# Delta rule: block products cut to the rows and columns that are read, and squares summed into rows

## The chip, the core and the metric

The kernel runs on one core of one Trainium2 chip. Its time is device time in microseconds (us). Five engines work side by side, each through its own instructions in order: TensorE (PE; its weight loads are listed apart as PEld), VectorE (DVE), ScalarE (ACT), GpSimd (POOL) and SyncE (SP), which here only sends weight loads. They wait for each other through semaphores. Lower is better.

## The reference, cut to what matters

One decoder layer, 256 tokens, width 2048, all in float32. A combined input projection feeds softmax attention (8 heads) and a gated delta rule (8 query/key heads, 16 value heads, head dimension 128); both are projected, merged by gates and projected out, then normalised, and a SwiGLU feed-forward follows. A conditioning vector gives six modulation vectors through a 2048 x 12288 weight, `w_ada`. Two parts concern the change:

```
qb = l2norm(q) * 128**-0.5 ;  kb = l2norm(k)         # x * rsqrt(sum(x*x) + 1e-6), per token and head
L  = strictly lower part of (k_beta k^T) * decay     # per head and chunk of the sequence
A  = L + I
u, w = solve(A, [v_beta, k_beta * exp(g_cum)])       # unit lower triangular
```

The kernel uses two chunks of 128 tokens per head and inverts `A` (128x128, unit lower triangular) outright.

## The kernel before, in words

**Weights.** All large products are the same routine: a 512 KB block of weights is loaded (`load_w`, L204, sent by SP), split into a rounded high part (`hi`, ScalarE, L211) and a remainder (`lo`, VectorE, L212), and multiplied three ways (L289 to L291, L337 to L339, L296 and L300). Loads go through four buffers called `raw`. The same four buffers also take the blocks of `w_ada` (`raw_a`, L240), which VectorE multiplies and sums (L229).

**Order.** The program is a list of such weight steps, up to three loaded ahead. After each step a small planner, `tick`, lets background work advance in four lanes ("moba", "main", "pre", "ada"): each is a generator that yields its estimated cost, and a tick spends 1.8 of it; `yield rest(n)` sets a lane aside for n ticks. What is given out this way fixes the program order, from which a scheduler writes each engine's stream at build time. On the chip each engine follows its stream.

**The delta rule's background work** comes in two batches `b` of 8 value heads. Lane "pre" runs, per batch, the short convolutions, then `gdn_qk`: squares of the 8 query and key heads (L577, ScalarE), their sums over the 128 channels as products with a column of ones (L580), an inverse square root (`rsqrt`, L347 to L353, six VectorE instructions and a ScalarE square root), a scale (L583), a transpose on TensorE (L587), a copy (L589), and a transfer to DRAM (`rnd`, L590, POOL's queue). It is read back as a broadcast over partitions (`rb`, L595) and multiplied in on VectorE (L597).

Lane "main" runs `gdn_chain`: masked score matrices `ma0`, `ma1` (L636 to L642); the inversion of the 32x32 diagonal blocks on VectorE in 31 steps; a trip through DRAM that spreads the inverted blocks over 128 partitions as `UU` (the inverse, transposed) and `TT` (the inverse), L678; and then `pair`, which combines the blocks, 32 to 64 to 128, for two heads and two chunks at a time, and applies the result to the values. A helper `four` issues four products (L691); there are five calls per pair: M times T, the two products with U, again M times T, and the last with U. In between VectorE scales by beta into `z` (L700, L712) and ScalarE copies the blocks that are read back into `TT` and `UU` with a minus sign (L706, L707, L716). There are 8 pairs in all (2 batches, 2 halves, 2 pairs), and the two pairs of a half take turns. A float32 product is two instructions on TensorE, each with its weight load.

Of the kernel before, what the change touches and what calls it, by code (L numbers as in the profile page):

```python
# [10 lines left out]
F32 = mybir.dt.float32  # L11
F32R = mybir.dt.float32r
AF = mybir.ActivationFunctionType
OP = mybir.AluOpType
# [4 lines left out]
P = 128  # L19
D = 2048  # L20
S = 256
# [11 lines left out]
SCALE = HD ** -0.5  # L33
# [3 lines left out]
O_Z, O_B, O_A = 7168, 9216, 9232  # L37
O_GA, O_GB = 9248, 11296

C_ID, C_MASK, C_BA, C_SUM, C_TRI, C_END = 0, 128, 256, 288, 289, 545  # L40
V_ADA, V_LNG, V_LNB, V_CONV, V_END = 0, 96, 112, 128, 256


def constants():
    c = np.zeros((P, C_END), np.float32)
    i = np.arange(P)
    c[:, C_ID:C_ID + P] = np.eye(P)
    c[:, C_MASK:C_MASK + P] = np.where(i[None, :] >= i[:, None], 0.0, NEG)
    c[i, C_BA + i % 32] = 1.0
    c[:, C_SUM] = 1.0  # L50
    c[:, C_TRI:C_TRI + P] = i[:, None] <= i[None, :]
    c[:, C_TRI + P:] = -(i[:, None] > i[None, :]).astype(np.float32)
    return c
# [39 lines left out]
def layer(ctx, tc, a, out):  # L93
    nc = tc.nc
    v_, s_, g_, t_, dma = nc.vector, nc.scalar, nc.gpsimd, nc.tensor, nc.sync
    sdma = nc.gpsimd
# [5 lines left out]
    pt = ctx.enter_context(tc.tile_pool(name="pt", bufs=2, space=PSUM))  # L102
# [8 lines left out]
    def e2(nm, shape):  # L111
        return k1.tile(shape, F32, tag="e2", name=nm, bufs=3)
# [5 lines left out]
    cw = cols[:, V_CONV:V_END]  # L118
    ident = cst[:, C_ID:C_ID + P]
    mask = cst[:, C_MASK:C_MASK + P]  # L120
    ones = cst[:, C_SUM:C_SUM + 1]

    def load_x(k0, kn):
        dma.dma_start(x_sb[:, k0:k0 + kn, :], a["xT"][:, k0:k0 + kn, :])
# [38 lines left out]
    def rest(n=1):  # L163
        return -n
# [181 lines left out]
    def rsqrt(dst, e, r, src, eps_col):  # L346
        v_.tensor_scalar(e, src, eps_col, None, op0=OP.add)  # L347
        s_.activation(r, e, AF.Sqrt)
        v_.reciprocal(r, r)
        v_.tensor_tensor(dst, r, r, op=OP.mult)  # L350
        v_.tensor_tensor(dst, dst, e, op=OP.mult)
        v_.tensor_scalar(dst, dst, -0.5, 1.5, op0=OP.mult, op1=OP.add)
        v_.tensor_tensor(dst, r, dst, op=OP.mult)  # L353
# [8 lines left out]
    def c2(nm, shape):  # L362
        return k1.tile(shape, F32, tag="c2", name=nm, bufs=4)
# [207 lines left out]
    def gdn_qk(b):  # L571
        kq = kqs[b]
        yield rest()
        ss = pg.tile([P, 512], F32, tag="gd", name="ss")
        for t in range(0, 8, 2):
            sq = e2("sq", [P, 2, S])
            s_.activation(sq, kq[:, t:t + 2, :], AF.Square)  # L577
            for i in range(4):
                n = 2 * t + i
                t_.matmul(ss[:, n:n + 1], sq[:, i // 2, i % 2 * P:(i % 2 + 1) * P], ones, start=True, stop=True)  # L580
        n16 = k1.tile([P, 3, 16], F32, tag="n16", name="n16")
        rsqrt(n16[:, 0], n16[:, 1], n16[:, 2], ss[:, :16], epsc[:, 0:1])
        v_.tensor_scalar(n16[:, 0, :8], n16[:, 0, :8], SCALE, None, op0=OP.mult)  # L583
        yield 1.2
        yield rest()
        tp = pt.tile([P, P], F32, tag="tp", name="tp")
        t_.transpose(tp[:16], n16[:, 0], ident)  # L587
        r = e2("rn", [16, P])
        s_.copy(r, tp[:16])  # L589
        sdma.dma_start(rnd[b].rearrange("t (h i) -> (t h) i", h=2), r)  # L590
        yield 0.1
        yield rest(2)
        for t in range(4):
            rb = e2("rb", [P, 2, S])
            sdma.dma_start(rb, bass.AP(tensor=rnd[b].tensor, offset=rnd[b].offset + t * S,  # L595
                                       ap=[[0, P], [4 * S, 2], [1, S]]))
            v_.tensor_tensor(kq[:, t::4, :], kq[:, t::4, :], rb, op=OP.mult)  # L597
            yield 0.6
# [14 lines left out]
    def gdn_chain(b):  # L613
# [61 lines left out]
        for hh in range(2):  # L675
            uu, tt = [k1.tile([P, 8, P], F32, tag="m4", name=x, bufs=3) for x in ("UU", "TT")]
            for w, dst in ((0, uu), (1, tt)):
                sdma.dma_start(dst, ubd[w][8 * hh:8 * hh + 8, :P, :].rearrange("u c i -> c u i"))  # L678
            yield rest(((9, 4), (20, 6))[b][hh])

            def pair(gq):
                hs = 4 * hh + 2 * gq
                us = slice(4 * gq, 4 * gq + 4)
                beta = bcs[:, 3:5, 8 * b + hs:8 * b + hs + 2].rearrange("p a h -> p h a")
                beta = beta.unsqueeze(3).to_broadcast([P, 2, 2, P])

                def four(lhs, rhs):
                    ps = pg.tile([P, 4, P], F32, tag="gd", name="ps4")
                    for n in range(4):
                        lt, rt = lhs(n), rhs(n)  # L690
                        t_.matmul(ps[:lt.shape[1], n, :], lt, rt, start=True, stop=True)  # L691
                    return ps

                def M(n):
                    return ma0[:, hs + n // 2, 1, 0:P] if n % 2 == 0 else ma1[:, hs + n // 2, 1, :]

                U, T = uu[:, us, :], tt[:, us, :]
                ps = four(M, lambda n: T[:, n, :])
                z = c2("z", [P, 4, P])
                v_.tensor_tensor(z.rearrange("p (h a) i -> p h a i", a=2),  # L700
                                 ps.rearrange("p (h a) i -> p h a i", a=2), beta, op=OP.mult)
                yield 0.6
                ps = four(lambda n: U[:, n, :], lambda n: z[:, n, :])
                ps2 = four(lambda n: z[:, n, :], lambda n: U[:, n, :])
                for lo, hi in ((slice(0, 32), slice(32, 64)), (slice(64, 96), slice(96, 128))):
                    s_.activation(T[hi, :, lo], ps[hi, :, lo], AF.Copy, scale=-1.0)  # L706
                    s_.activation(U[lo, :, hi], ps2[lo, :, hi], AF.Copy, scale=-1.0)  # L707
                yield 0.1
                lo, hi = slice(0, 64), slice(64, 128)
                ps = four(M, lambda n: T[:, n, :])  # L710
                z = c2("z", [P, 4, 64])
                v_.tensor_tensor(z[hi].rearrange("p (h a) i -> p h a i", a=2),  # L712
                                 ps[hi, :, lo].rearrange("p (h a) i -> p h a i", a=2), beta[hi, :, :, lo], op=OP.mult)
                yield 0.35
                ps = four(lambda n: z[hi, n, :], lambda n: U[hi, n, :])
                s_.activation(U[lo, :, hi], ps[lo, :, hi], AF.Copy, scale=-1.0)  # L716
                yield 0.1

                hp = slice(hs, hs + 2)
                vn = c2("vn", [P, 2, 2, P])  # L720
                ps = pg.tile([P, 2, P], F32, tag="gd", name="pv0")
                for i in range(2):
                    t_.matmul(ps[:, i, :], U[:, 2 * i, :], bv[:, 0, hs + i, :], start=True, stop=True)
                s_.copy(vn[:, 0], ps)
                ps = pg.tile([P, 2, P], F32, tag="gd", name="pr1")
                for i in range(2):
                    t_.matmul(ps[:, i, :], ma0[:, hs + i, 1, P:S], vn[:, 0, i, :], start=True, stop=True)
                for i in range(2):
                    hd = 8 * b + hs + i
                    v_.scalar_tensor_tensor(bv[:, 1, hs + i, :], ps[:, i, :], nb[:, 1, hd:hd + 1], bv[:, 1, hs + i, :],  # L730
                                            op0=OP.mult, op1=OP.add)
                yield 0.4
                ps = pg.tile([P, 2, P], F32, tag="gd", name="pv1")
                for i in range(2):
                    t_.matmul(ps[:, i, :], U[:, 2 * i + 1, :], bv[:, 1, hs + i, :], start=True, stop=True)
                s_.copy(vn[:, 1], ps)
                po = pg.tile([P, 2, 2, P], F32, tag="gd", name="po")
                for i in range(2):
                    t_.matmul(po[:, 0, i, :], ma0[:, hs + i, 0, 0:P], vn[:, 0, i, :], start=True, stop=True)
                for i in range(2):  # L740
                    t_.matmul(po[:, 1, i, :], ma0[:, hs + i, 0, P:S], vn[:, 0, i, :], start=True, stop=False)
                    t_.matmul(po[:, 1, i, :], ma1[:, hs + i, 0, :], vn[:, 1, i, :], start=False, stop=True)
                s_.copy(bv[:, :, hp, :], po)
                yield 0.3

            pairs = [pair(0), pair(1)]
            while pairs:
                for x in list(pairs):
                    try:
                        yield next(x)  # L750
                    except StopIteration:
                        pairs.remove(x)
                yield rest()
# [490 lines left out]
```

## Time and profile before

| | |
|---|---|
| median of 3 runs | 1789.39 us (1779.66 to 1791.91) |
| the profiled execution | 1785.36 us |
| its span, first to last instruction | 1783.6 us |
| mean granted TensorE clock | 0.983 |
| ScalarE, POOL busy | 815.2 us (46%), 49.9 us (3%) |
| HBM read | 412.27 MB |

The profile is of one execution. "Busy" counts the time in which an engine has an instruction in work; matmuls are pipelined, so one lasts longer than the step to the next. An engine's idle time matters only where something on the chain of waits hangs on it. The granted clock is a share of 2.4 GHz; 0.5 is 1.2 GHz.

### The profile page before, as it was taken

The page shows a single profiled execution, that of the slowest core. Times are in us where ns is not written, and L with a number is a line of the kernel's source. Part 1 is how long each engine was busy: PE and PEld are TensorE (multiplying, and loading weights), DVE is VectorE, ACT ScalarE, POOL GpSimd, SP SyncE. Part 2 cuts the span into 40 slices and gives each one's busy share as a digit, 9 for nine tenths or more (in the row PEclk, how much of TensorE's full clock was granted, in tenths as well). Part 3 has the DMA queues.
Part 4 walks back from the last instruction along what each step waited for, and adds up shares of the span by engine and source line. Part 5 has one row for each costly group of instructions (what it writes and reads, how often), then busy time and mean ns, then how long its engine had stood idle before and what let it go on. Part 6 is the DMA issues. An engine that isn't in the chain of part 4 may idle for free.

```text
span 1783.6 us, 28261 instructions
## 1 busy us (share of the span) xinstructions
PE 1686.6 (95%) x11149; PEld 1537.1 (86%) x11149; DVE 1249.9 (70%) x1786; ACT 815.2 (46%) x1118; POOL 49.9 (3%) x68
## 2 busy tenths in 40 slices
PE   3899999999989999899999899999999999999995
PEld 3899999979989788889998899888888888888895
DVE  6899988888856787657875677676666655455454
ACT  3544445667433445336344344544444444433342
POOL 0000000110100001000000000000000000000001
PEclk9999999999999999999999999999999999999998
DMA  9999887666677577876876647777777755765652
GB/s 356 331 339 353 345 310 227 199 196 189 205 238 238 186 237 247 271 239 206 296 265 222 191 129 245 251 252 239 238 246 232 242 193 192 258 197 188 197 185 82
DMA packets 115158, 421.56 MB, mean 236 GB/s; under 512 B 13456, under 2 KB 14384, under 8 KB 109392
## 3 DMA queue, kind: packets, MB, share of 16 engines
q1 hardware_dynamic: 110016, 402.21, 66.7%
q0 software_dynamic: 5008, 17.53, 3.7%
q8 instruction: 88, 1.44, 0.3%
q14 instruction: 46, 0.38, 0.1%
HBM read 412.27 MB, written 7.42 MB: 235 GB/s over the span
## 4 chain that ended last, share of the span: by engine, by line
PE 41%; issue 15%; DMA 8%; DVE 5%; ACT 1%; POOL 0%; POOLq 0%; DVEq 0%; ACTq 0%
PE mm L296 16%; PE mm L300 8%; DMA raw_a<-in_w_ada 4%; DVE lo L212 3%; PE mm L290 3%; PE mm L291 3%; PE mm L289 3%; PE mm L339 2%; PE mm L338 2%; PE mm L337 2%; DMA raw<-in_w_proj_gdn 2%; DMA raw<-in_w_in 1%; ACT hi L211 1%; PE ps L691 1%; DMA rb<-rnd 1%
## 5 line engine op out<-in xcount | busy, mean ns | idle before, releaser
L211 ACT CAST hi<-raw 128x1024 fp32r<-128x1024 f32 (+2 forms) x572 | 582.0, 1020 | 768.7 <-PE mm L339 210.7
L212 DVE TENSOR_TENSOR lo<-raw,hi 128x1024 fp32r<-128x1024 f32 (+2 forms) x572 | 672.8, 1183 | 286.1 <-ACT hi L211 282.1
L289 PE MATMUL mm<-s,hi 128*128 128x256 f32 x1184 | 338.9, 286 | 4.9 <-ACT hi L211 4.7
L291 PE MATMUL mm<-s,lo 128*128 128x256 f32 x1184 | 333.3, 283 | 6.3 <-DVE lo L212 6.2
L290 PE MATMUL mm<-s,hi 128*128 128x256 f32 x1184 | 332.5, 281 | 0.0
L296 PE MATMUL mm<-h,hi 128*128 128x512 f32 x1280 | 319.0, 391 | 0.0
L296 PEld LDWEIGHTS mm<-h,hi 128*128 128x128 f32 x1280 | 228.8, 188 | 39.5
L289 PEld LDWEIGHTS mm<-s,hi 128*128 128x128 f32 x1184 | 225.0, 190 | 10.8 <-ACT hi L211 7.5
L291 PEld LDWEIGHTS mm<-s,lo 128*128 128x128 f32 x1184 | 224.2, 190 | 9.4 <-DVE lo L212 8.5
L290 PEld LDWEIGHTS mm<-s,hi 128*128 128x128 f32 x1184 | 224.8, 190 | 0.4
L300 PEld LDWEIGHTS mm<-h,lo 128*128 128x128 f32 x1280 | 171.1, 188 | 13.2
L300 PE MATMUL mm<-h,lo 128*128 128x256 f32 x1280 | 174.1, 278 | 0.0
L337 PE MATMUL mm<-hi,ach 128*128 128x512 f32 (+1 forms) x440 | 152.6, 347 | 0.0
L338 PE MATMUL mm<-lo,ach 128*128 128x512 f32 (+1 forms) x440 | 152.5, 347 | 0.0
L339 PE MATMUL mm<-hi,acl 128*128 128x512 f32 (+1 forms) x440 | 152.5, 347 | 0.0
L229 DVE CUSTOM_DVE_ANT_0 raw_a<-raw_a,cb,cols 128x1024 f32<-128x1024 f32 x56 | 71.8, 1283 | 77.9 <-DMA raw_a<-in_w_ada 77.9
L229 DVE CUSTOM_DVE_ANT_0 raw_a<-raw_a,cb,ada_half 128x1024 f32<-128x1024 f32 x56 | 71.8, 1283 | 64.8 <-DMA raw_a<-in_w_ada 64.8
L229 DVE CUSTOM_DVE_ANT_0 r<-r,cb,cols 128x2048 f32<-128x2048 f32 x40 | 93.7, 2347 | 14.1 <-DMA r<-in_w_ada 14.1
L337 PEld LDWEIGHTS mm<-hi,ach 128*128 128x128 f32 x440 | 83.3, 189 | 10.4
L339 PEld LDWEIGHTS mm<-hi,acl 128*128 128x128 f32 x440 | 83.3, 189 | 10.4
L338 PEld LDWEIGHTS mm<-lo,ach 128*128 128x128 f32 x440 | 83.3, 189 | 10.1
L338 PE MATMUL mm<-lo,s 128*128 128x512 f32 x192 | 77.0, 401 | 2.2 <-DVE lo L212 2.2
(288 smaller groups left out, 2383.2 us busy)
## 6 DMA issues: line engine op xcount, KB each, us to landing
raw<-in_w_ffn_in SPq DMA_DIRECT2D x176, 512.0 KB, 4.3
raw<-in_w_in SPq DMA_DIRECT2D x168, 512.0 KB, 4.4
raw_a<-in_w_ada SPq DMA_DIRECT2D x112, 512.0 KB, 4.5
raw<-in_w_ffn_out SPq DMA_DIRECT2D x88, 512.0 KB, 4.3
r<-in_w_ada SPq DMA_DIRECT2D x40, 1024.0 KB, 7.6
raw<-in_w_proj_gdn SPq DMA_DIRECT2D x32, 512.0 KB, 4.5
raw<-in_w_out SPq DMA_DIRECT2D x32, 512.0 KB, 4.2
raw<-in_w_in SPq DMA_DIRECT2D x40, 384.0 KB, 5.8
```

The lines of the kernel that those rows point to most:

```text
L211: s_.copy(hi, raw)
L212: v_.tensor_tensor(lo, raw, hi.bitcast(F32), op=OP.subtract)
L229: v_.tensor_tensor_reduce(out=raw, in0=raw, in1=cb[:, n * part:n * part + n], scale=1.0, scalar=cols[:, col:col + 1] if first else h, op0= ...
L289: t_.matmul(o, hi[:, i, c], ah, start=(first and i == 0 and t == 0), stop=False)
L290: t_.matmul(o, hi[:, i, c], al, start=False, stop=False)
L291: t_.matmul(o, lo[:, i, c], ah, start=False, stop=(last and i == kn - 1 and t == 1))
L296: t_.matmul(box[t].rearrange("p (u i) -> p u i", u=2), hi[:, i, t * P:(t + 1) * P], both[k0 + i], start=(first and i == 0), stop=False)
L300: t_.matmul(box[t][:, :S], lo[:, i, t * P:(t + 1) * P], both[k0 + i][:, 0, :], start=False, stop=(last and i == kn - 1))
L337: t_.matmul(box[h], xh, hi[:, i, :], start=start, stop=False)
L338: t_.matmul(box[h], xh, lo[:, i, :], start=False, stop=False)
L339: t_.matmul(box[h], xl, hi[:, i, :], start=False, stop=stop)
L691: t_.matmul(ps[:lt.shape[1], n, :], lt, rt, start=True, stop=True)
```

## The change

Two places. In `gdn_qk` the sums of squares no longer use the squares as weights and one column of ones as moving data. The weights are now 8 columns of the constants, of which the one for head n is all ones (a window of a block of 15 columns that slides), and the squares of a head, 256 tokens, move; eight products add into one 8x256 tile, so the sums stand as rows. `rsqrt` then works on 8 partitions of 256 elements, the result goes to DRAM without transpose and copy, and one rest of the lane falls away.

In `pair` every product is restricted to the rows and columns that are read afterwards. The first, third and last calls compute 32 or 64 columns for the 32 or 64 partitions that matter; the pair of products with U works on 32x32 blocks. The planner's cost of the first step is 0.55 instead of 0.6.

```diff
-C_ID, C_MASK, C_BA, C_SUM, C_TRI, C_END = 0, 128, 256, 288, 289, 545
+C_ID, C_MASK, C_BA, C_SEL, C_TRI, C_END = 0, 128, 256, 288, 303, 559
-    c[:, C_SUM] = 1.0
+    c[:, C_SEL + 7] = 1.0
...
     def gdn_qk(b):
-        ss = pg.tile([P, 512], F32, tag="gd", name="ss")
+        ss = pg.tile([8, S], F32, tag="gd", name="ss")
         for t in range(0, 8, 2):
             sq = e2("sq", [P, 2, S])
             s_.activation(sq, kq[:, t:t + 2, :], AF.Square)
-            for i in range(4):
-                n = 2 * t + i
-                t_.matmul(ss[:, n:n + 1], sq[:, i // 2, i % 2 * P:(i % 2 + 1) * P], ones, start=True, stop=True)
-        n16 = k1.tile([P, 3, 16], F32, tag="n16", name="n16")
-        rsqrt(n16[:, 0], n16[:, 1], n16[:, 2], ss[:, :16], epsc[:, 0:1])
-        v_.tensor_scalar(n16[:, 0, :8], n16[:, 0, :8], SCALE, None, op0=OP.mult)
-        yield 1.2
-        yield rest()
-        tp = pt.tile([P, P], F32, tag="tp", name="tp")
-        t_.transpose(tp[:16], n16[:, 0], ident)
-        r = e2("rn", [16, P])
-        s_.copy(r, tp[:16])
-        sdma.dma_start(rnd[b].rearrange("t (h i) -> (t h) i", h=2), r)
-        yield 0.1
+            for n in (t, t + 1):
+                t_.matmul(ss, cst[:, C_SEL + 7 - n:C_SEL + 15 - n], sq[:, n - t, :], start=(n == 0), stop=(n == 7))
+        rn = e2("rn", [8, S])
+        rsqrt(rn, e2("rne", [8, S]), e2("rnr", [8, S]), ss, epsc[:8, 0:1])
+        v_.tensor_scalar(rn[:4], rn[:4], SCALE, None, op0=OP.mult)
+        sdma.dma_start(rnd[b], rn)
+        yield 1.9
         yield rest(2)
...
-                def four(lhs, rhs):
-                    ps = pg.tile([P, 4, P], F32, tag="gd", name="ps4")
+                def four(lhs, rhs, to=slice(0, P), w=P):
+                    ps = pg.tile([P, 4, w], F32, tag="gd", name="ps4")
                     for n in range(4):
-                        lt, rt = lhs(n), rhs(n)
-                        t_.matmul(ps[:lt.shape[1], n, :], lt, rt, start=True, stop=True)
+                        t_.matmul(ps[to, n, :], lhs(n), rhs(n), start=True, stop=True)
                     return ps
...
-                ps = four(M, lambda n: T[:, n, :])
-                z = c2("z", [P, 4, P])
-                v_.tensor_tensor(z.rearrange("p (h a) i -> p h a i", a=2),
-                                 ps.rearrange("p (h a) i -> p h a i", a=2), beta, op=OP.mult)
-                yield 0.6
-                ps = four(lambda n: U[:, n, :], lambda n: z[:, n, :])
-                ps2 = four(lambda n: z[:, n, :], lambda n: U[:, n, :])
-                for lo, hi in ((slice(0, 32), slice(32, 64)), (slice(64, 96), slice(96, 128))):
-                    s_.activation(T[hi, :, lo], ps[hi, :, lo], AF.Copy, scale=-1.0)
-                    s_.activation(U[lo, :, hi], ps2[lo, :, hi], AF.Copy, scale=-1.0)
+                q = [slice(32 * n, 32 * n + 32) for n in range(4)]
+                ps = pg.tile([P, 4, 32], F32, tag="gd", name="ps_mt")
+                for n in range(4):
+                    for lo, hi in ((q[0], q[1]), (q[2], q[3])):
+                        t_.matmul(ps[hi, n, :], M(n)[:, hi], T[:, n, lo], start=True, stop=True)
+                z = c2("z", [P, 4, 32])
+                for hi in (q[1], q[3]):
+                    v_.tensor_tensor(z[hi].rearrange("p (h a) i -> p h a i", a=2),
+                                     ps[hi].rearrange("p (h a) i -> p h a i", a=2), beta[hi, :, :, 0:32], op=OP.mult)
+                yield 0.55
+                ps = pg.tile([P, 2, 4, 32], F32, tag="gd", name="ps_a")
+                for n in range(4):
+                    t_.matmul(ps[q[1], 0, n, :], U[q[1], n, q[1]], z[q[1], n, :], start=True, stop=True)
+                    t_.matmul(ps[q[0], 1, n, :], z[q[1], n, :], U[q[1], n, q[1]], start=True, stop=True)
+                s_.activation(T[q[1], :, q[0]], ps[q[1], 0], AF.Copy, scale=-1.0)
+                ps2 = four(lambda n: z[q[3], n, :], lambda n: U[q[3], n, q[3]], q[2], 32)
+                s_.activation(U[q[0], :, q[1]], ps[q[0], 1], AF.Copy, scale=-1.0)
+                s_.activation(U[q[2], :, q[3]], ps2[q[2]], AF.Copy, scale=-1.0)
                 yield 0.1
                 lo, hi = slice(0, 64), slice(64, 128)
-                ps = four(M, lambda n: T[:, n, :])
+                ps = four(lambda n: M(n)[:, hi], lambda n: T[:, n, lo], hi, 64)
...
-                ps = four(lambda n: z[hi, n, :], lambda n: U[hi, n, :])
-                s_.activation(U[lo, :, hi], ps[lo, :, hi], AF.Copy, scale=-1.0)
+                ps = four(lambda n: z[hi, n, :], lambda n: U[hi, n, hi], lo, 64)
+                s_.activation(U[lo, :, hi], ps[lo], AF.Copy, scale=-1.0)
```

## Rows read from the trace of the kernel before

**Rows 1.** The page, busy us, share of the span and instructions of each engine.

```profile
PE 1686.6 (95%) x11149; PEld 1537.1 (86%) x11149; DVE 1249.9 (70%) x1786; ACT 815.2 (46%) x1118; POOL 49.9 (3%) x68
```

**Rows 2.** The page, the chain that ended last: shares of the span by engine.

```profile
PE 41%; issue 15%; DMA 8%; DVE 5%; ACT 1%; POOL 0%; POOLq 0%; DVEq 0%; ACTq 0%
```

**Rows 3.** The chain of waits, 480 to 820 us, shares of that stretch by line.

```profile
by line: DMA raw_a<-in_w_ada 18.6%; DVE lo L212 9.9%; issue 7.7%; DMA raw<-in_w_in 6.6%; PE mm L289 5.2%; PE mm L290 5.2%; PE mm L291 5.0%; PE ps L691 3.3%; DMA rb<-rnd 3.2%; DVE Ub L666 2.5%; DVE tm L664 2.4%; ACT hi L211 2.3%; PE mm L339 
```

**Rows 4.** Stretches: busy us of each engine, granted clock, DMA share, GB/s.

```profile
core 0: us, PE busy (x) PEld busy (x) DVE busy (x) ACT busy (x) POOL busy (x), PEclk, DMA share, GB/s
336.00:344.00 8.00, 8.00 (x42) 7.82 (x41) 3.67 (x10) 1.49 (x5) 0.47 (x1) 0.57 0.83 245
364.00:367.00 3.00, 0.13 (x3) 0.00 (x1) 1.78 (x4) 0.36 (x1) 1.45 (x3) 0.99 0.61 242
367.00:371.00 4.00, 4.00 (x12) 3.30 (x13) 3.60 (x7) 2.79 (x7) 0.38 (x1) 0.58 0.83 210
372.00:490.00 118.00, 114.35 (x843) 106.87 (x842) 106.78 (x222) 77.57 (x107) 10.70 (x13) 1.00 0.61 192
491.00:495.00 4.00, 4.00 (x38) 4.00 (x37) 2.43 (x3) 1.28 (x2) 0.00 (x0) 1.00 1.01 326
502.00:505.00 3.00, 0.00 (x0) 0.00 (x0) 2.90 (x11) 1.05 (x1) 0.00 (x0) 1.00 0.76 210
524.00:532.00 8.00, 8.00 (x41) 7.52 (x42) 4.54 (x6) 0.76 (x2) 0.00 (x0) 0.58 0.66 195
576.00:582.00 6.00, 6.00 (x52) 5.70 (x50) 2.43 (x3) 2.19 (x4) 0.37 (x1) 1.00 0.80 254
```

**Rows 5.** Timeline of TensorE: start us, length us, the one-column products.

```profile
332.50 2.74 PE L580 MATMUL ss<-cst,sq 128*128 128x1 f32 x24
```

**Rows 6.** Timeline, norms and what waits; in brackets idle before and releaser.

```profile
346.22 0.17 DVE L583 TENSOR_SCALAR n<-n 128x8 f32<-128x8 f32 x1
355.09 0.51 POOL L590 DMA_DIRECT2D rnd<-rn  x1 [11.02 <-ACT rn L589]
364.56 0.69 DVE L597 TENSOR_TENSOR kq<-kq,rb 128x512 f32<-128x512 f32 x1 [5.63 <-DMA rb<-rnd]
505.07 0.28 PE L587 MATMUL tp<-cst,n 128*16 128x128 f32 x1 [3.21 <-DVE n L583]
505.93 0.53 POOL L590 DMA_DIRECT2D rnd<-rn  x1 [15.84 <-ACT rn L589]
523.95 3.68 PE L691 MATMUL ps<-UU,z 64*64 64x128 f32 x16 [3.97 <-DVE z L712]
```

**Rows 7.** The chain of waits around 601 us: start, length, piece.

```profile
601.05 0.86 PE g L636 x2
```

**Rows 8.** VectorE by line and shape: busy us, mean ns, idle before.

```profile
L349 DVE RECIPROCAL n<-n 128x16 f32<-128x16 f32 x2 | 0.5, 248 | 0.0
L498 DVE RECIPROCAL bcs<-w 128x32 f32<-128x32 f32 x1 | 0.4, 352 | 0.0
L700 DVE TENSOR_TENSOR z<-ps,bcs 128x512 f32<-128x512 f32 x8 | 5.2, 683 | 0.0
L712 DVE TENSOR_TENSOR z<-ps,bcs 64x256 f32<-64x256 f32 x8 | 3.4, 428 | 0.6 <-PE ps L691 0.3
```

**Rows 9.** Timeline of TensorE: products of a pair, and the weight product behind.

```profile
508.69 1.06 PE L691 MATMUL ps<-z,UU 128*128 128x128 f32 x8
509.58 1.06 PE L691 MATMUL ps<-UU,z 128*128 128x128 f32 x8
...
801.74 1.08 PE L691 MATMUL ps<-UU,z 64*64 64x128 f32 x8 [0.63 <-DVE z L712]
802.76 0.38 PE L289 MATMUL mm<-s,hi 128*128 128x256 f32 x1
```

**Rows 10.** Weight loads by line and shape: busy us, mean ns, idle before.

```profile
L691 PEld LDWEIGHTS ps<-TT,ma 128*128 128x128 f32 x128 | 15.0, 192 | 0.0
L432 PEld LDWEIGHTS ps_ba<-hf,wba 128*32 128x32 f32 x32 | 1.5, 111 | 24.6 <-ACT hf L429 23.6
```

More of the change, by code (lines that the diff above doesn't have):

```diff
@@ L120, in layer @@
     mask = cst[:, C_MASK:C_MASK + P]
-    ones = cst[:, C_SUM:C_SUM + 1]
     def load_x(k0, kn):
@@ L708, in pair @@
+                s_.activation(U[q[0], :, q[1]], ps[q[0], 1], AF.Copy, scale=-1.0)
+                s_.activation(U[q[2], :, q[3]], ps2[q[2]], AF.Copy, scale=-1.0)
                 yield 0.1
                 lo, hi = slice(0, 64), slice(64, 128)
-                ps = four(M, lambda n: T[:, n, :])
+                ps = four(lambda n: M(n)[:, hi], lambda n: T[:, n, lo], hi, 64)
                 z = c2("z", [P, 4, 64])
                 v_.tensor_tensor(z[hi].rearrange("p (h a) i -> p h a i", a=2),
-                                 ps[hi, :, lo].rearrange("p (h a) i -> p h a i", a=2), beta[hi, :, :, lo], op=OP.mult)
+                                 ps[hi].rearrange("p (h a) i -> p h a i", a=2), beta[hi, :, :, lo], op=OP.mult)
```

## The prediction

> **What bounds the kernel now.** I read the page's busy table first: TensorE is busy 95% of the span, VectorE 70% [rows 1]. That share doesn't say what a microsecond of TensorE is worth here, so I went to the chain of waits. It is 41% TensorE, 8% transfers, 5% VectorE and 15% "issue" of the span [rows 2]. The delta rule's combination runs between 500 and 815 us; cut to 480 to 820 us, the chain is led by `w_ada` transfers with 18.6%, and the term to see is "PE ps L691", the products being rewritten: 3.3% of 340 us, 11.2 us on the chain [rows 3].
>
> Then the windows table: granted clock and TensorE's busy time in single stretches [rows 4]. Three things are to be seen. At 336 us the clock falls to half for most of 8 us though TensorE was never idle; what ran just before is 24 one-column products, 2.74 us long [rows 5]. At 364 and 520 us TensorE is idle for 3 and 4 us, and after each the clock is at 1.2 instead of 2.4 GHz for a while (mean 0.58 over 4 and 8 us). At 502 us it is idle for 3 us with no fall.
>
> The waits name the cause of the idle times [rows 6]. At 364 us VectorE has waited 5.63 us for `rb`, the broadcast read of the norms; the norms were only sent at 355.09 because their transpose sat a tick later on TensorE. At 505.07 the transpose itself waited 3.21 us for VectorE, holding all products behind it. At 523.95 the last products of a pair wait 3.97 us for `z`, queued on VectorE behind four multiplies that waited for `rb`.
>
> **The change part by part.**
>
> *Squares (twice, batch 0 and 1).* Removed: 16 products of one column, 32 instructions at 2.74/24 = 0.115 us, 3.7 us. Added: 8 products with 256 columns moving and 8 columns of weights, 16 instructions. A float product with 512 moving columns takes 0.86 us for its two instructions, 0.43 each [rows 7], so 256 columns cost 0.21: 3.4 us. That is -0.3 us each. The larger part is the clock: 8 us at 0.57 cost 8 x 0.43 = 3.4 us in batch 0. In batch 1 the same products left the clock at 1.00 [rows 4], so this is not certain; bounds are 0 and -3.4, and I take -3.4, because a full-rate stream takes the place of the one-column one and TensorE was busy on both sides of the fall. The Trainium skill, "TensorE: Matmul & The Clock Gate", section on the HAM oscillation, ties the fall to idle gaps of the engine; by that rule the fall at 336 us would belong to something else and this term would be 0. The row, busy at 100% before the fall, speaks against it.
>
> *Transpose, copy and one rest removed.* The norms go to DRAM as soon as VectorE has them. Batch 0: VectorE had them at 346.4, the old path sent them 8.7 us later [rows 6]. VectorE's work grows: the reciprocal took 0.248 us on 16 and 0.352 us on 32 elements [rows 8], 6.5 ns an element, so 1.8 us on 256; the six others at most 0.43 us by the row of 256 elements, in all 4.4 us against at most 7 x 0.25 = 1.7, so +2.7 us per batch. In batch 0 it is hidden by the 5.63 us in which VectorE waits anyway. The norms then leave at about 349, and the multiply (9.5 us behind the sending in the old path) could start near 358.5, where VectorE now begins to wait (364.56 - 5.63 = 358.9). On POOL's queue the sending stands ahead of the `rb` reads as before. So the idle 3 us at 364 and the 4 x 0.42 = 1.7 us of half clock after it go: -4.7 us. What is late next is the weight cast, one step ahead of its use. Bounds: 0 (the multiplies move forward by as much as the transfer does) and -4.7.
>
> Batch 1: the transpose's wait of 3.21 us on TensorE goes, but VectorE was busy for 2.90 of those 3 us [rows 4] and the weight products behind need its subtractions: I count a third, -1.0. Against it the norms leave at 505.93 + 2.7 - 0.7 for the two hops saved = 507.9, 2 us later; that transfer is on the chain, with `z`, the weight subtractions and a POOL load (`TT`) queued behind: +2.0. Net +1.0, bounds -3 and +4.
>
> *Block products.* Per pair 40 instructions now: 32 of 128x128 at (509.58 - 508.69)/8 = 0.111 us, and 8 of 64x64 that take 802.76 - 801.74 = 1.02 us with the change of shape, 0.13 us more than eight of the others [rows 9]. Together 4.6 us, for 8 pairs 37. Afterwards 56 instructions: 40 with 32 columns on both sides, 16 with 64. No row has both short. The upper end is 0.111 (one moving column still stepped at 0.115, so the weights' 128 columns set it); the lower is those columns' share, 0.028 for 32 and 0.055 for 64. A load of 32 columns lasts 0.111 us against 0.192 [rows 10], so length does fall with columns; I take 0.065, near the middle. 56 x 0.065 = 3.6 us, plus four changes of shape at 0.13 = 4.1. That saves 0.5 us per pair, 4 us in all; the ends are 40 x 0.028 + 16 x 0.055 = 2.0 us (saves 2.1 a pair with the shape changes, 17 us) and 6.2 + 0.5 = 6.7 us (costs 17 us). On the chain lie 11.2 of 37 us, 30%: -1.2, between -5 and +5. The same skill page, section "Back-to-back issue gap", gives 25 ns or 62 ns as least spacing, depending on the decode path. By 62 ns the pair would be 3.5 us, by 25 ns near my lower end; no row here shows either.
>
> *The rest.* `z` goes from one operation of 0.683 us to two of 128 elements, about 0.30 each by the two rows for 512 and 256 [rows 8]; ScalarE drops one of four copies per pair. VectorE waits there for `raw_a` (first on the chain, [rows 3]), which hides the 0.08 us per pair: 0; without that cover -0.6 us. The constants grow by 14 columns: nothing.
>
> **Sum:** -3.7 - 0.3 - 4.7 + 1.0 - 1.2 = -8.9 us. The profiled execution took 1785.4 us, so 1776.5; the median of the runs shown is 4.0 us higher and would give 1780.5. I predict 1779.
>
> **Rivals.**
> 1. *Absorbed.* The gains end at the next `w_ada` transfer or weight cast; only a part of the batch 0 terms stays: 0 to -4, 1782 to 1789. For it: transfers lead the chain from 480 on [rows 3]. Against: from 372 to 490 us TensorE is busy for 114 of 118 us at full clock [rows 4], so what batch 0 gains should arrive at 490. Chance 0.20.
> 2. *Short products are no shorter.* At 0.111 us each the pairs cost 17 us more of TensorE, a third to all of it on the chain: +5 to +17 in place of -1.2: 1785 to 1797. For it: the one-column row. Chance 0.10.
> 3. *Slower: the clock.* The one-column products preceded a fall with TensorE "busy"; a 32x32 product is a sixteenth of a 128x128 one, and if bursts of them do the same, each of three bursts in four half-groups costs 3.4 us: 12 x 3.4 = 41, less 9: 1817. It decides once more than 8 of the 12 bursts are followed by half clock. Against: the 64x64 products at 574 us are followed by a clock of 1.00 from 576 to 582 [rows 4], and weight products stand between the bursts. Chance 0.06.
> 4. *More.* With one rest fewer the `rb` wait at 520 us falls away too: 4.0 idle and 8 x 0.42 = 3.4 of half clock; and at the low price of the products, half of their 17 us counts, 7 more than summed: 1779 - 7.4 - 7 = 1765. For it: all of these stalls stand in line behind one transfer. Against: VectorE sends later in batch 1. Chance 0.14.
>
> My forecast has the remaining 0.50, with its own range of 1773 to 1784. The change not doing what it says is rival 2.
>
> **Numbers.** One per cent, about what a measurement of this kernel can tell from no change, is 18 us: faster means below 1771.5, slower above 1807.3 against the median. Faster: rival 4 and a little of the forecast, 0.15. Slower: rival 3, 0.06. Within: 0.79. Range 1763 to 1797, which takes in rivals 1, 2 and 4 and leaves out rival 3 and tails.
>
> **What would show it.** Right: no half clock at 336-344 us; POOL sends the norms of batch 0 before 351 us and VectorE's first `rb` wait there is under 3 us; the transpose's line is gone; the reciprocal lasts about 1.8 us; steps of the new products at 0.05 to 0.08 us, with whole pairs on TensorE near 4 us instead of 4.6. Wrong: a clock under 0.9 behind the bursts, steps of 0.11 us, an `rb` wait in batch 1 over 6 us, or a batch 0 stretch that is as long as before because `lo` or a weight transfer ends it.

## The result: 1776.6 us, half a per cent faster

The changed kernel takes 1776.57 us in the median of 14 runs (1771.03 to 1782.33), the kernel before 1786.18 in 14 runs beside them. The ratio is 0.9948, 95% interval 0.9935 to 0.9961: 9.3 us less at 1785 us. The sum said -8.9. The profiled execution took 1772.32 us, with a span of 1770.3. That the sum is right to half a microsecond is chance, as the experiments show: the products were wrong by 17 us and the rest of the sum by 16, in opposite directions. Below, a ratio is turned into microseconds as (ratio - 1) x 1785. By the intervals given, one such figure is uncertain by 2 to 4 us, and the difference of two by some 4.

The busy line and the chain by engine of the changed kernel, to be held against [rows 1] and [rows 2]:

```profile
PE 1665.7 (94%) x11243; PEld 1509.8 (85%) x11243; DVE 1256.1 (71%) x1794; ACT 814.7 (46%) x1109; POOL 50.3 (3%) x68
...
PE 37%; issue 16%; DMA 6%; DVE 5%; ACT 1%; POOL 0%; POOLq 0%; ACTq 0%; DVEq 0%
```

TensorE lost 20.9 us of busy time, over twice what the time gained. The next view shows where the products lost it: TensorE by line and shape (busy us, mean ns of one, idle before), first the five calls of `pair` in the changed kernel, then the lines of the kernel before that they replace.

```profile
L682 PE MATMUL ps<-TT,ma 128*64 128x64 f32 x64 | 5.8, 261 | 0.1
L682 PE MATMUL ps<-UU,z 64*64 64x64 f32 x64 | 4.6, 221 | 1.2 <-DVE z L711 1.2
L682 PE MATMUL ps<-UU,z 32*32 32x32 f32 x64 | 3.8, 203 | 0.7 <-DVE z L696 0.7
L702 PE MATMUL ps_a<-UU,z 32*32 32x32 f32 x64 | 3.8, 202 | 0.0
L693 PE MATMUL ps_mt<-TT,ma 128*32 128x32 f32 x128 | 2.8, 197 | 1.7 <-DMA TT<-ubd 1.7
```

```profile
L691 PE MATMUL ps<-TT,ma 128*128 128x128 f32 x128 | 15.7, 275 | 0.0
L691 PE MATMUL ps<-z,UU 128*128 128x128 f32 x64 | 10.8, 321 | 7.7 <-DVE z L700 7.5 <-ACT TT L706 0.2
L691 PE MATMUL ps<-UU,z 64*64 64x128 f32 x64 | 9.9, 311 | 4.7 <-DVE z L712 4.6
L691 PE MATMUL ps<-UU,z 128*128 128x128 f32 x64 | 9.8, 304 | 0.0
```

Before it is 46.2 us. After, 20.8 in these lines and 3.7 in the other half of `ps_a` (L701): 24.5 together, 21.7 less. A mean of 200 ns is the length of one instruction, though, not the step to the next; the steps come from the timeline of TensorE in the changed kernel:

```profile
499.91 0.70 PE L693 MATMUL ps_mt<-TT,ma 128*32 128x32 f32 x32
554.31 0.41 PE L682 MATMUL ps<-UU,z 32*32 32x32 f32 x8 [0.23 <-DVE z L696]
511.99 1.15 PE L682 MATMUL ps<-TT,ma 128*64 128x64 f32 x16
517.31 1.14 PE L682 MATMUL ps<-UU,z 64*64 64x64 f32 x16 [1.15 <-DVE z L711]
```

32 instructions of `ps_mt` end 0.70 us after the first starts; less the length of one, (0.70 - 0.197) / 31 = 0.016 us a step. Eight 32x32 ones that all go to the same 32 partitions step at (0.41 - 0.203) / 7 = 0.030, the 64-column ones at about (1.15 - 0.22) / 15 = 0.062. `ps_a` alternates its output partitions as `ps_mt` does; its 16 instructions at 505.75 us take 0.44 us, (0.44 - 0.20) / 15 = 0.016 too. The steps of a pair are 32 x 0.016 + 8 x 0.030 + 16 x 0.062 = 1.7 us. For the old shapes the same count gives 40 x 0.111 = 4.4, and the prediction had 3.6 for the new ones; its 4.6 and 4.1 hold the changes of shape as well.

The other half of the story is in the windows. These are the stretches of batch 0 in the kernel before, where the rows ahead of the prediction did not look (TensorE, its loads, VectorE, ScalarE, POOL busy; granted clock; DMA share; GB/s):

```profile
344.00:360.00 16.00, 16.00 (x133) 15.78 (x132) 13.99 (x35) 10.89 (x22) 2.74 (x5) 1.00 0.65 218
360.00:368.00 8.00, 5.13 (x37) 4.81 (x36) 2.78 (x5) 2.24 (x5) 1.82 (x3) 0.93 0.71 226
416.00:440.00 24.00, 21.98 (x178) 21.10 (x177) 18.32 (x43) 20.20 (x32) 1.67 (x2) 1.00 0.57 179
344.00:488.00 144.00, 137.48 (x1005) 128.55 (x1004) 126.22 (x269) 93.12 (x138) 13.60 (x19) 0.99 0.62 196
```

And the same stretches of the changed kernel, with that of the old half clock first:

```profile
336.00:344.00 8.00, 8.00 (x63) 7.14 (x62) 4.97 (x11) 5.65 (x8) 0.00 (x0) 1.00 0.73 230
...
344.00:360.00 16.00, 8.93 (x69) 8.37 (x67) 10.46 (x25) 5.16 (x11) 3.70 (x6) 0.93 0.67 216
360.00:368.00 8.00, 8.00 (x50) 7.88 (x50) 6.15 (x14) 5.66 (x14) 1.32 (x3) 0.70 0.43 118
416.00:440.00 24.00, 19.55 (x163) 19.03 (x162) 19.09 (x50) 18.69 (x31) 2.24 (x3) 1.00 0.51 149
344.00:488.00 144.00, 130.57 (x945) 122.07 (x944) 122.92 (x261) 87.23 (x132) 16.36 (x21) 0.98 0.60 186
```

The half clock at 336 us is gone, the idle 2.9 us at 364 too. But TensorE is now idle for 7.1 us between 344 and 360, where it had been busy throughout, and 2.4 us longer between 416 and 440. Over batch 0's 344 to 488 us its idle time went from 6.5 to 13.4 us. The timeline of the changed kernel says on what it waits (in brackets the idle time and its releaser):

```profile
341.35 1.28 DVE L228 CUSTOM_DVE_ANT_0 raw_a<-raw_a,cb,ada_half 128x1024 f32<-128x1024 f32 x1 [2.96 <-DMA raw_a<-in_w_ada]
342.83 1.73 DVE L348 RECIPROCAL rnr<-rnr 8x256 f32<-8x256 f32 x1
349.24 0.53 POOL L582 DMA_DIRECT2D rnd<-rn  x1 [14.78 <-DVE e L622]
352.34 0.49 PE L822 MATMUL psS<-qk 128*128 128x128 f32 x2 [2.79 <-DVE ya L217]
358.53 0.69 DVE L589 TENSOR_TENSOR kq<-kq,rb 128x512 f32<-128x512 f32 x1 [5.19 <-DMA rb<-rnd]
359.33 0.29 DVE L838 TENSOR_SCALAR pe<-pe,st 128x128 f32<-128x128 f32 x1
359.67 0.47 PE L848 MATMUL tp<-cst,pe 128*128 128x128 f32 x1 [4.28 <-DVE pe L838]
434.56 0.70 PE L855 MATMUL poa<-pT,tv 128*128 128x256 f32 x2 [3.35 <-ACT pT L850]
```

The norms left at 349.24 and the multiply with `rb` ran at 358.53, both as predicted to within 0.3 us. Only VectorE's wait did not shrink (5.63 to 5.19): the multiply itself had moved a tick forward in VectorE's stream. In the kernel before, this wait stood ahead of `ya` (L218), and TensorE waited for that:

```profile
367.00 0.80 PE L823 MATMUL psS<-qk 128*128 128x128 f32 x2 [2.87 <-DVE ya L218]
```

Now it stands ahead of `pe` (L838), the division in the softmax of the attention that TensorE needs for the transposes of its next products, and TensorE waits 4.28 us in place of 2.87. The 2.79 us before it come from `ya` (L217), which VectorE delivers late; VectorE itself had waited 2.96 us for a block of `w_ada` (`raw_a`) at 341.35, in front of the reciprocal.

### The profile page after: what moved, and what is told of

Read it like the earlier page. It is cut to its first block, busy times and chain, and to the rows that moved or that the text cites. A ratio compares the mean times of both kernels' runs of the same rounds, so it can differ in the third digit from the quotient of the medians.

```text
span 1770.3 us, 28430 instructions
## 1 busy us (share of the span) xinstructions
PE 1665.7 (94%) x11243; PEld 1509.8 (85%) x11243; DVE 1256.1 (71%) x1794; ACT 814.7 (46%) x1109; POOL 50.3 (3%) x68
## 4 chain that ended last, share of the span: by engine, by line
PE 37%; issue 16%; DMA 6%; DVE 5%; ACT 1%; POOL 0%; POOLq 0%; ACTq 0%; DVEq 0%
PE mm L295 17%; PE mm L299 8%; DVE lo L211 3%; DMA raw<-in_w_in 2%; PE mm L338 2%; PE mm L337 2%; PE mm L336 2%; PE mm L289 2%; PE mm L290 2%; PE mm L288 2%; DMA raw<-in_w_proj_gdn 2%; DMA raw_a<-in_w_ada 1%; ACT hi L210 1%; DVE raw_a L228 0%; DVE Ub L658 0%
## 5 line engine op out<-in xcount | busy, mean ns | idle before, releaser
L336 PE MATMUL mm<-hi,s 128*128 128x512 f32 x192 | 78.4, 410 | 1.5 <-ACT hi L210 1.5
```

Of the source, the lines that this page charges most:

```text
L336: t_.matmul(box[h], xh, hi[:, i, :], start=start, stop=False)
```

## Experiments

The change has three parts that can be parted: the products, the squares' work, and the order (one rest of the lane lost, the sending a tick earlier). The order part also books the squares at a cost of 1.9 in place of 1.2 and 0.1, where a tick spends 1.8; "the lost rest" below is both, and no run parts them. All runs were compared with the kernel before.

**Products alone.** The kernel before with the new `pair`; squares, transpose and rests as before.

```diff
-                ps = four(M, lambda n: T[:, n, :])
+                ps = pg.tile([P, 4, 32], F32, tag="gd", name="ps_mt")
...
```

> The block products are cut, the squares stay as before. Theory A (the gain comes from the block products, whose step fell to about 0.016 us and so took some 24 us off TensorE): -7 to -11 us against before, nearly the whole gain. Theory B (the prediction's sum: squares and the earlier norms carry 8 of 9 us): -1 to -3 us. The clock at about 336 us falls to half again under both, if one-column products cause the fall.

1767.16 us, ratio 0.9899 (0.9881 to 0.9917): 18.0 us faster, twice the whole change and more than either theory had. That is the full 17 us that the prediction's lowest price gives and a little more, with no discount for what lies off the chain. The gain arises where the pairs run: VectorE's 157th `lo` (of 572, one for each weight block) comes at 470.6 us, before at 469.7; the 241st at 784.1, before at 804.5.

**Squares alone**, with the lost rest: the changed kernel with the old block of `pair`.

```diff
-                ps = pg.tile([P, 4, 32], F32, tag="gd", name="ps_mt")
+                ps = four(M, lambda n: T[:, n, :])
...
```

> The squares are summed by selector columns and a rest falls away, the block products stay wide. Theory A: between -2 and +2 us against before. Theory B: -7 to -9 us. Both: no half clock right behind the squares of batch 0, a reciprocal of 1.74 us, and an `rb` wait of VectorE of about 5 us that has only moved forward.

1792.3 us, 1.0036 (1.0022 to 1.0051): 6.4 us slower, which neither theory had. So this half of the change costs time, though it removes instructions.

**The lost rest alone.** The kernel before, with nothing but the two yields and the rest taken as in the changed kernel; the transpose stays.

```diff
-        yield 1.2
-        yield rest()
         tp = pt.tile([P, P], F32, tag="tp", name="tp")
...
-        yield 0.1
+        yield 1.9
```

> Before, with only the planner's yields of the squares changed (1.9 in place of 1.2, a rest and 0.1); same instructions, another order. Theory A: within 3 us of before, since order alone gives nothing. Rival C (what was gained is the order, one rest fewer): -5 to -10 us. The one-column products stay, so a fall of the clock behind them in batch 0 is expected again.

1795.97 us, 1.0053 (1.0035 to 1.0072): 9.5 us slower, with the same 11149 instructions on TensorE and 1786 on VectorE. Neither expectation had a loss. Two of the three stalls of the changed kernel are there, on the same releasers:

```profile
359.79 0.47 PE L847 MATMUL tp<-cst,pe 128*128 128x128 f32 x1 [4.12 <-DVE pe L837]
...
435.56 0.70 PE L854 MATMUL poa<-pT,tv 128*128 128x256 f32 x2 [4.09 <-ACT pT L849]
```

The wait for `ya` at 352 us is not; the reciprocal is still the short one here (L349 in [rows 8]), and VectorE doesn't wait for `raw_a` ahead of it.

**The changed kernel with one rest more ahead of the reads.**

```diff
-        yield rest(2)
+        yield rest(3)
```

> The changed kernel with three rests in place of two ahead of the `rb` reads, so that the multiplies stand one tick later in VectorE's stream. If the 5.2 us in which VectorE waits for `rb` in batch 0, the idle TensorE behind it and the half clock after it are on the path: -3 to -6 us against the changed kernel (-13 to -16 against before), and the wait under 3 us. If what batch 0 gains is taken back later: within 2 us of the changed kernel.

1770.33 us, 0.9923 (0.9902 to 0.9944), 4.5 us below the changed kernel by the ratios, hardly more than the intervals can tell. The multiplies go back a tick, and of the two stalls at 350 us the one behind `rb` nearly vanishes, while the one for `ya` stays:

```profile
352.92 0.76 PE L822 MATMUL psS<-qk 128*128 128x128 f32 x2 [2.75 <-DVE ya L217]
361.63 0.70 PE L848 MATMUL tp<-cst,pe 128*128 128x128 f32 x3 [0.79 <-DVE pe L838]
```

**Both parts with the old order.** The changed kernel; the sending stays a rest behind the norms.

```diff
+        yield 1.2
+        yield rest()
         sdma.dma_start(rnd[b], rn)
-        yield 1.9
+        yield 0.1
```

> The changed kernel with the planner's yields of the squares as before: 1.2, a rest, the sending, 0.1. If the lost rest alone is what the squares cost (the products alone gave -18 us, the lost rest alone +11): -18 to -22 us against before, as fast as the products alone or faster by the 3 us of half clock. If the row layout itself costs (2.7 us more on VectorE per batch): -12 to -16 us.

1760.55 us, 0.987 (0.985 to 0.9889): 23.2 us faster than before and 13.9 faster than the change, further than expected. It is the best version of this study; of both kernels it keeps the new work and the old order. Its windows for the same stretches:

```profile
344.00:360.00 16.00, 16.00 (x134) 15.82 (x133) 11.24 (x29) 8.00 (x18) 4.29 (x7) 1.00 0.60 187
360.00:368.00 8.00, 3.16 (x18) 2.77 (x17) 6.76 (x14) 4.42 (x10) 0.38 (x1) 0.81 0.64 197
416.00:440.00 24.00, 24.00 (x203) 23.84 (x202) 21.67 (x50) 20.23 (x35) 1.67 (x2) 1.00 0.63 202
344.00:488.00 144.00, 137.86 (x1007) 129.42 (x1006) 126.80 (x265) 91.78 (x138) 15.37 (x20) 0.98 0.62 195
```

TensorE is busy throughout from 344 to 360 and from 416 to 440 us. Over 344 to 488 us it is idle for 6.1 us, against 13.4 in the changed kernel. It pays 4.84 us at 366 us, more than the kernel before, and still comes out ahead. The reciprocal is the long one here too, but there is no wait for `ya`: the block of `w_ada` ahead of the reciprocal comes with hardly a wait.

```profile
336.88 1.28 DVE L228 CUSTOM_DVE_ANT_0 raw_a<-raw_a,cb,ada_half 128x1024 f32<-128x1024 f32 x1 [0.42 <-DMA raw_a<-in_w_ada]
340.37 1.74 DVE L348 RECIPROCAL rnr<-rnr 8x256 f32<-8x256 f32 x1 [0.38 <-ACT rnr L347]
366.05 1.22 PE L857 MATMUL poa<-pT,tv 128*128 128x256 f32 x2 [4.84 <-ACT pT L852]
```

**The squares' work with the old order**, and the old products: the changed kernel with both edits.

```diff
+        yield 1.2
+        yield rest()
         sdma.dma_start(rnd[b], rn)
-        yield 1.9
+        yield 0.1
...
-                ps = pg.tile([P, 4, 32], F32, tag="gd", name="ps_mt")
+                ps = four(M, lambda n: T[:, n, :])
...
```

> Wide block products, squares by selector columns, the planner's yields as before. Lost rest to blame: -4 to 0 us against before. Row layout to blame: +2 to +6 us, with VectorE's reciprocals of 1.74 us ahead of weight subtractions.

1781.46 us, 0.9987 (0.9973 to 1.0): 2.3 us faster, with no change at the edge of the interval. So the new squares are worth some 2 us alone and, by 0.9899 to 0.987, 5 on top of the new products, each hardly more than the intervals can tell. The lost rest on top of them costs 1.0036 - 0.9987, 8.7 us.

**Products alone, padded.** The first version, with 24 wide instructions of the old shape added per pair ahead of the small ones; their results are overwritten.

```diff
+                def wide():
+                    big = pg.tile([P, 4, P], F32, tag="gd", name="big")
+                    for n in range(4):
+                        t_.matmul(big[:, n, :], M(n), T[:, n, :], start=True, stop=True)
+                    return big
-                ps = pg.tile([P, 4, 32], F32, tag="gd", name="ps_mt")
+                ps = wide()[:, :, 0:32]
...
```

> The block products alone (as e1), and ahead of three of the five groups four wide products M times T into the same tile, whose result is overwritten: 24 instructions of 128x128 per pair, 2.7 us, so that a pair takes about 4.3 us of TensorE as before. If TensorE's time in the pairs is what counts: the gain of 18 us shrinks to 0 to 5. If it was the shorter hops on VectorE and ScalarE or the order: it stays at 12 to 18.

1785.74 us, 1.0003 (0.9989 to 1.0017). The busy time of TensorE rose from 1672.0 to 1695.7 us, by 23.7; the time by 18.6. Within the 2.5 us of the interval the whole gain is gone, though the smaller VectorE multiplies and the dropped copy are in the padded version too: what gained was TensorE's time in the pairs. By these two busy times it counts at 18.6 / 23.7 = 78%. The share is rough: from the kernel before to the products alone the busy time fell by 14.6 us and the time by 18.0, and the padded version is as fast as the kernel before with 9.1 us more of busy time. So a few microseconds may come from something else; no run parts them.

```profile
PE 1672.0 (95%) x11277; PEld 1520.8 (86%) x11277; DVE 1251.2 (71%) x1794; ACT 811.8 (46%) x1110; POOL 49.8 (3%) x68
```

```profile
PE 1695.7 (95%) x11469; PEld 1541.7 (86%) x11469; DVE 1248.2 (70%) x1794; ACT 812.7 (46%) x1110; POOL 49.9 (3%) x68
```

The first line is the products alone, the second the padded version.

**Both with the old order, sums as 32 rows of 64.** Four times as many selector products, each a quarter as wide; VectorE then works on 64 elements a partition, not 256.

```diff
-        ss = pg.tile([8, S], F32, tag="gd", name="ss")
+        ss = pg.tile([32, 64], F32, tag="gd", name="ss")
...
-                t_.matmul(ss, cst[:, C_SEL + 7 - n:C_SEL + 15 - n], sq[:, n - t, :], start=(n == 0), stop=(n == 7))
+            for n in range(4 * t, 4 * t + 8):
+                t_.matmul(ss, cst[:, C_SEL + 31 - n:C_SEL + 63 - n], sq[:, n // 4 - t, n % 4 * 64:n % 4 * 64 + 64],
+                          start=(n == 0), stop=(n == 31))
```

> As e5, with the sums laid out as 32 rows of 64 (a window of 63 selector columns, 32 products with 64 columns moving), so the reciprocal falls from 1.74 to about 0.55 us and VectorE's work for the norms from about 4 to 2 us per batch. If that work is on the path: 2 to 5 us faster than e5. If not: within 1.5 us of e5.

1766.29 us, 0.9898 (0.9881 to 0.9915): 5.0 us slower than the version with both and the old order, hardly more than the intervals can tell, where 2 to 5 faster was expected. The reciprocal did fall from 1.74 to 0.54 us, and the first multiply with `rb` came at 352.31 us instead of 357.58. That it lost all the same is not explained: the scheduler ordered other work differently as well, and no run here parts the two. The trace shows only where: the 157th `lo` comes at 470.9 us against 467.7 in the version with both, the 169th at 522.6 against 513.2.

**The old order in one batch only.** Batch 0 keeps the rest, batch 1 does not, and the mirror of it.

```diff
+        if b == 0:
+            yield 1.2
+            yield rest()
         sdma.dma_start(rnd[b], rn)
-        yield 1.9
+        yield 0.1 if b == 0 else 1.9
```

> The changed kernel with the old plan of the norms' step (cost 1.2, one rest, sending, cost 0.1) in batch 0 alone; batch 1 keeps the new one. Theory L (what the lost rest costs is one stall of batch 0, the attention products at 434 us that come a tick early and wait for the copy of pT): at the sigmoid near 500 us the changed kernel is 12.6 us behind the version with both rests, and at 585 us 14.5, so batch 0 holds some 13 of 16 us: 1762 to 1765, the pT wait under 1 us. Theory M (either batch costs half): about 1768. Theory N (batch 1 holds it): 1775 to 1778.

> The mirror: the old plan in batch 1 alone. Theory L: 1772 to 1776, the pT wait near 434 us still 3 to 4 us. Theory M: about 1768. Theory N: 1760 to 1763. If the two batches' shares don't add up to 16 us, the order of one depends on the other's.

Batch 0: 1764.3 us, 0.9887 (0.987 to 0.9903). Batch 1: 1771.4 us, 0.9922 (0.9901 to 0.9943). Against the changed kernel that is -10.9 and -4.6 us; together 15.5, where both at once gave 13.9. So the cost lies about two thirds in batch 0, and theory L has the larger share right. The wait for `pT` near 435 us is gone with batch 0's rest and still 3.37 us without it, as that theory has it, but it was one stall of three. TensorE's waits at 340 to 370 us, in batch 0 kept, then in batch 1 kept:

```profile
365.11 0.72 PE L858 MATMUL poa<-pT,tv 128*128 128x256 f32 x2 [3.86 <-ACT pT L853]
```

```profile
356.06 0.80 PE L825 MATMUL psS<-qk 128*128 128x128 f32 x2 [2.79 <-DVE ya L217]
363.01 0.47 PE L851 MATMUL tp<-cst,pe 128*128 128x128 f32 x1 [2.45 <-DVE pe L841]
```

With batch 0's rest both early stalls are gone and one later one is left; without it they are back. VectorE's 169th `lo` comes at 511.2 us here and at 513.2 in the version with both rests, where batch 0 keeps its rest; in the changed kernel and the mirror it comes at 526.5 and 529.0. The rest of batch 1 is worth 4.6 us by the mirror and 3.0 by 0.9887 to 0.987, about what the intervals can tell, and no single stall was found for it. The two traces can't show it: the mirror's profiled execution took 1776.68 us, the changed kernel's 1772.32, the other way round from their medians.

**The best version with a rest more ahead of the reads.**

```diff
         yield 0.1
-        yield rest(2)
+        yield rest(3)
```

> The version with both rests, with one more tick ahead of the broadcast reads (rest(3) in place of rest(2)). In that version VectorE still waits 4.58 us for rb in batch 0. If that wait matters, 2 to 4 us below that version's 1760.6: 1757 to 1759. If what matters is only where a tick puts the attention pieces of batch 0, this shifts them again, to either side: 1758 to 1772; above 1766 it speaks for the order and against the wait.

1770.91 us, 0.9923 (0.9907 to 0.9939): 9.5 us slower than without it. VectorE's first wait for `rb` did fall, from the first of these rows (the best version) to the second:

```profile
357.58 0.69 DVE L591 TENSOR_TENSOR kq<-kq,rb 128x512 f32<-128x512 f32 x1 [4.58 <-DMA rb<-rnd]
```

```profile
359.70 0.69 DVE L591 TENSOR_TENSOR kq<-kq,rb 128x512 f32<-128x512 f32 x1 [1.50 <-DMA rb<-rnd]
```

3 us of wait less and 9.5 us of time more: the length of that wait was not what mattered. TensorE's idle time from 344 to 488 us went from 6.1 to 12.3 us. The same extra rest gained 4.5 us in the changed kernel.

## Why the prediction came out right, point by point

By the ratios the change is: products -18.0, squares' work -5.2 on top of them, lost rest +13.9, in all -9.3. The prediction had -1.2, and -7.7 for squares and order together with their signs mixed. The total was right, two steps were not.

- *Squares.* Right in its row: 336 to 344 us runs at 1.00. 16 instructions took 3.4 us by prediction; the selector products' busy time for both batches is 7.2 us, 3.6 each. The price of -4.0 for both batches lies between the -2.3 and -5.2 that the runs give for the squares' whole work, transpose and longer `rsqrt` included.
- *Transpose, copy and rest.* This step failed, in taking -4.7 from two bounds that both excluded a loss: the rest that falls away costs 8.7 to 13.9 us. The multiply moved forward by as much as the transfer did, which the prediction had as its bound of 0; but what it moved ahead of, the softmax's division, was not looked for. "What is late next is the weight cast" was wrong: it was the attention. The other new stall, `ya`, shows near 352 us in the four traces with the new squares and no rest in batch 0 (2.75 to 2.86 us). In just these four VectorE has waited 2.95 to 3.03 us for a block of `w_ada` in front of the reciprocal; in the five with the new squares and that rest it waited 0.17 to 0.42 us there, and of these three have no wait for `ya` at that place and two have 0.35 and 1.18 us. So that stall takes the order and the new squares together, and the late block goes with it; that the longer VectorE work alone would bring it is not shown, and the three traces speak against it. Batch 1's net +1.0 had the bounds -3 and +4; its rest is worth 3.0 to 4.6 us.
- *Block products.* This step failed twice, both times too careful. The step was taken as 0.065 us, between 0.028 and 0.111; measured are 0.016, 0.030 and 0.062. The products that don't alternate their output partitions are near the lower bound, the share of their columns (0.028 and 0.055), so the middle was the wrong choice; those that alternate take half of that, and the pair's 1.7 us is below the lower bound of 2.0. And the 30% from the chain of waits was the wrong measure: most of TensorE's time there counts, 78% by the padded version. A likely reason, not tried: the lines of [rows 3] name only what ended last, and behind a product that is not on the chain stands, on the same engine, a weight product that is.
- *The skill's rule.* The Trainium skill, "TensorE: Matmul & The Clock Gate", section "Back-to-back issue gap", gives 25 ns as the least spacing of small products, or 62 ns by the other decode path. No row here shows 62 for 32 columns: 30 ns where the outputs share their 32 partitions is near the first figure, and 16 ns, where they alternate, is below it.
- *Rivals.* Rival 2 (no shorter) fell, and rival 3 (half clock behind the bursts) too: the mean clock from 495 to 820 us is 0.97 in both kernels. Rival 4 (more) had the low price of the products right, and even half of it counting was too little; in batch 1 the wait for `z` did shrink, from 3.97 [rows 6] to 1.15 us, but the lost rest cost more in batch 0 than it gained there. Rival 1, absorbed, is near in time but has the wrong reason: the gains were not absorbed, they were paid back by new waits in batch 0.
- *What would show it.* The clock, the sending before 351 us, the missing transpose and the reciprocal (1.73 us against 1.8) came as written. The `rb` wait under 3 us (5.19), the steps of 0.05 to 0.08 and the pair near 4 us did not. Of the signs of being wrong, the `rb` wait in batch 1 stayed at 3.46 us. The clock did fall beside two of the bursts, to a mean of 0.57 from 508 to 512 and from 559 to 563 us, each time after TensorE had been idle for 2 us.

What stays open: what batch 1's rest is worth and why, why 32 rows of 64 lose, and how much of the lost rest's 8.7 to 13.9 us belongs to each stall. TensorE's idle time from 344 to 488 us grew with it in every setting: 6.5 to 9.9 us in the kernel before, 4.7 to 11.1 with the new squares, 6.1 to 13.4 with both parts.

## What to carry to other kernels

On an engine that is busy 95% of the time, as here, count most of a saving of its time (78% by the padded version), and don't discount it by its share of the chain. Where an edit moves a step by a tick, list what stands behind the moved instruction on its engine, and who waits for that, before counting the wait that goes: here one lost rest cost from about half to three quarters of what the products saved. When a change has a part that saves work and a part that moves it, time the two apart: the saving with the old order was 23 us, not 9.

## What was not expected of the hardware

Small products whose outputs alternate between partitions step at 0.016 us, those on the same 32 partitions at 0.030, against 0.062 for 64 columns and 0.111 for 128x128 ones [rows 9]. Without alternation the step is about 0.9 ns a column; with it, two take what one takes alone. No run changed the output partitions alone. The reciprocal follows its elements in a partition, 248 ns for 16 [rows 8], 542 for 64, 1738 for 256. And the half clock behind the one-column products, with TensorE busy 8.00 of 8 us, is not a rule: of eight such places in four traces with the old squares (two batches each) it followed in four. Two of these stretches, products alone in batch 0, then in batch 1:

```profile
336.00:344.00 8.00, 8.00 (x43) 7.82 (x42) 3.87 (x11) 1.74 (x4) 0.54 (x1) 0.59 0.78 248
...
496.00:504.00 8.00, 8.00 (x44) 8.00 (x43) 4.12 (x8) 2.25 (x3) 0.00 (x0) 0.57 0.87 301
```

In the padded version the same place in batch 0 stayed at 1.00. From 336 to 344 us, with the new products, it was 1.00 in all nine versions that have them. In batch 1 it fell to half beside them in three of the nine, each time with a wait of TensorE for the squares between the products (2.65, 5.79 and 5.87 us). What sets it was not tried.
